# A hybrid decoder trunk on one core: one group of low weight parts on GpSimd, values ahead of the forget gates' transposes, two residual tiles kept, one PSUM buffer and one addition moved

## The chip, the cores and the metric

The kernel runs on one core of a Trainium2 chip. The metric is the device time of one execution in microseconds. Instruction streams of TensorE (PE; PEld is its weight loads), VectorE (DVE), ScalarE (ACT), GpSimd (POOL) and SyncE (SP) run side by side; SyncE and GpSimd issue the DMAs here, each in the order of its queue.

## The reference

Two layers on a sequence of 1024 tokens of width 1024, batch 1, all float32, and a norm at the end. Cut to what matters:

```python
def reference(x, ...):
    for i in range(2):
        h = rms_norm(x, norm_g[i])
        x = x + (lru_mixer(h, ...) if i % 2 == 0 else fox_mixer(h, ...))
    return rms_norm(x, final_g)

def lru_mixer(h, ...):            # width 1536, 12 blocks of 128 channels
    u = h @ w_in                  # branch and gate
    xc = causal_conv(branch)      # 4 taps
    a, b = gates(xc)              # block-diagonal 128x128 products, sigmoids
    y = scan(a, b) * silu(gate)   # h[t] = a[t] h[t-1] + b[t]
    return y @ w_out

def fox_mixer(h, ...):            # 16 heads of 64
    q, k, v, gate, f = split(h @ w_in)
    cum = cumsum(log_sigmoid(f + b_f))
    logits = q k^T / 8 + cum[q] - cum[k], causal
    return (softmax(logits) v * silu(gate)) @ w_out
```

## The kernel before, in words

Products are made of split numbers: a high part and a low part of each operand, and three products (high x high, high x low, low x high) into one PSUM tile. The first layer splits in float32r, the second in float16. The sequence is worked in two halves of 512 tokens (`halves`, `HALF`); a channel block has 128 rows, so a tile of the residual `x` is 128x512.

**First layer**, until about 417 us. Twelve blocks pass through the input products, the convolution, the gates, the scan (`a`), and `outputs`, which makes `yh` and `yl`. Pairs of blocks are projected out by `project_out(g)`. `out_weights` (L396) loads 128x512 weights, has ScalarE make the high part `wh` (`to_hi`) and VectorE the low part `wl` (`to_lo`, L114). Most other low parts of this layer (46 tiles) are made by GpSimd, also in L114.

**The passage** between the layers (about 395 to 500 us, from L670). The last pair's weights are made by four calls of `out_weights`; then for each half the eight residual tiles get their last products (`ops`, L688 adds them to `x`), are stored to `x1d` in DRAM, squared for the norm, and split into the float16 tiles `h` that the second layer's products read. The row of the norm comes by way of small TensorE products (`sscol`, `rsrow`, `xnorm`). Between these, the scheduler places the first products of the second layer: `gps` (queries and keys, gates) and `vps` (values, L798 takes them to `v`). Its order is made by a planner that simulates the program (`schedule_with_timeline_sim`); for a stretch, ScalarE and VectorE keep the order of the code (`manual_schedule`, L1019). The generator `first` gives the values of pair group 0; `take(first, n)` runs n steps of it. The generator `forget` computes the log of the forget gates (`z`, L990), transposes it on TensorE (`fps`, L76), makes the running sum (L998) and stores `decay` rows that the attention loads into `T` and `U`.

**Attention**, about 500 to 976 us. Per head: `S` (scores, TensorE), a masked maximum (L1097, VectorE), exponential (ScalarE), scaling (L1110), a DMA transpose of the probabilities (`pT<-pp`, L1112), `O` (probabilities by values). The order strings at the top say where other work is laid between; from about 887 us this is `partial` (L1256), which multiplies the finished pairs by the output weights, four and two blocks at a time, and adds the residual read back from `x1d` (L1271). `home` (L1241) says where the sum lives: tiles `xh` that stay in SBUF, or, for `db < 3` of the second half (`c == 1`), a pair of buffers `R` (`xp`), from which it goes back to `x1d` (L1273) and is read again at the end (`x1`). Before a load into a buffer that stays, GpSimd copies one column of a tile two steps back (L1266), which makes the load wait for that tile's addition.

**The end** (`turned`, L1302). The residual tiles are transposed into PSUM (`turn`), the last two pairs' output products are added, squares are summed (`ssq`), VectorE multiplies by the gain (L1341), and `root_mean` gives the factor of the norm. For the last rows the gain's product of the last part is issued inside `root_mean` by `between` (L1347). PSUM tiles come from tags with two buffers each: `S`, `g`, `O`; a tile waits until the buffer two allocations back is read.

Of the kernel before, what the change touches and what calls it, by code (L numbers as in the profile page):

```python
# [11 lines left out]
F32 = mybir.dt.float32  # L12
# [5 lines left out]
ALU = mybir.AluOpType  # L18

P = 128  # L20
SEQ = 1024
HALF = 512
KT = 8
NB = 12
# [14 lines left out]
def f32(ap):  # L39
    return ap.bitcast(F32)  # L40
# [3 lines left out]
def trunk(ctx: ExitStack, tc: tile.TileContext, xt, w0, wg, wo0, pc, gn, gf, w1, wv, wf, bf, wo1, out):  # L44
    nc = tc.nc

    def pool(name, bufs, **kw):
        return tc.tile_pool(name=name, bufs=bufs, **kw)
# [5 lines left out]
    ps = ctx.enter_context(pool("ps", 2, space=PSUM))  # L54
# [16 lines left out]
    def matmul(*args, **kw):  # L71
        pe[0] = nc.tensor.matmul(*args, **kw)  # L72
        return pe[0]
# [26 lines left out]
    def to_hi(hi, src, eng, scale=None):  # L100
        if eng is nc.scalar:
            if scale is None:
                cast_last[0] = nc.scalar.copy(hi, src)
            else:
                nc.scalar.activation(hi, src, AF.Copy, scale=scale)
        elif eng is nc.gpsimd:
            nc.gpsimd.tensor_scalar(hi, src, 1.0 if scale is None else scale, 0.0, ALU.mult, ALU.add)
        elif scale is None:
            eng.tensor_copy(hi, src)
        else:  # L110
            eng.tensor_scalar(hi, src, scale, None, ALU.mult)

    def to_lo(lo, src, hi, eng):
        return eng.tensor_tensor(lo, src, f32(hi), ALU.subtract)  # L114
# [3 lines left out]
    def loaded(shape):  # L118

        if spare and next(loads) % 4 == 3:  # L120
            return spare[0].tile([P, *shape], F32, tag="wx", name="wf")
        return wpool.tile([P, *shape], F32, tag="wf", name="wf", bufs=3)
# [30 lines left out]
    def drain(gen):  # L153
        for _ in gen:
            pass

    def take(gen, n):
        for _ in range(n):
            next(gen, None)
# [48 lines left out]
    with nullcontext(ExitStack()) as l0:  # L208
# [43 lines left out]
        first = ([], [])  # L252
# [140 lines left out]
                to_lo(yl, a_, yh, nc.vector)  # L393
            ys.append(y)

        def out_weights(g, d0):  # L396

            wt = loaded([4, P])
            for j in range(2):
                nc.sync.dma_start(wt[:, 2 * j : 2 * j + 2], wo0[d0 + j, :, 2 * g : 2 * g + 2])  # L400
            hi = wpool.tile([P, 4, P], F32R, tag="wh", name="wh")
            lo = wpool.tile([P, 4, P], F32R, tag="wl", name="wl")
            to_hi(hi, wt, nc.scalar)
            to_lo(lo, wt, hi, nc.vector)
            return [[(hi[:, 2 * j + i], lo[:, 2 * j + i]) for i in range(2)] for j in range(2)]

        def project_out(g):
# [76 lines left out]
        for n in range(NB):  # L484
# [3 lines left out]
            else:  # L488
                ups = two_banks("ups")
                both = [ups.rearrange("p a b -> p (a b)")]  # L490
# [61 lines left out]
        rpool = late.enter_context(pool("R", 2, side="right"))  # L552
# [116 lines left out]

        weight_bounds()  # L670
        splitting = iter(())
        wl = [w for d0 in range(0, KT, 2) for w in out_weights(NB // 2 - 1, d0)]
        for h, cs in enumerate(halves):
            y = [tuple(z[:, cs] for z in p) for p in ys[-2:]]
            hT[h] = [hpool.tile([P, 2, HALF], FP16, tag="hh", name="h16") for k in range(KT)]
# [2 lines left out]
            for d0 in range(0, KT, 4):  # L678
# [6 lines left out]
                for db, o in enumerate(pts, d0):  # L685
                    mm3(o, wl[db][1], y[1], False, True)
                    x = xs[h][db]
# [28 lines left out]
    with ExitStack() as l1:  # L716
# [298 lines left out]
        first = values(0)  # L1015
# [26 lines left out]
        one = onesf[:HEADS, :1].to_broadcast([HEADS, HALF])  # L1042
        gates0 = forget(0)
        next(gates0)
        take(first, 3)
        drain(gates0)
        drain(first)
        gw = [None]
# [195 lines left out]
        def home(c, db):  # L1244
            if c == 0:
                x = hpool.tile([P, HALF], F32, tag="hh", name="xh")
            elif db < 3:
                return rpool.tile([P, HALF], F32, tag="R", name="xp")
            elif db < 7:
                x = at.tile([P, HALF], F32, tag="wv", name="xh", bufs=4)  # L1250
            else:
                x = at.tile([P, HALF], F32, tag="wvf", name="xh", bufs=1)
            homes[c, db] = x
            return x
# [24 lines left out]
        def residual(c, q):  # L1279

            cs = slice(q * 256, (q + 1) * 256)
            xs = [homes[c, d][:, cs] if (c, d) in homes else None for d in range(KT)]
            for d in range(0, KT, 2):
                n = xs[d : d + 2].count(None)
                if n:
                    x = wpool.tile([P, 2, 256], F32, tag=("wl", "wh")[q], name="x1")
                    fetch(x[:, :n], x1d[c, :, d : d + n, cs])
                    xs[d : d + n] = [x[:, i] for i in range(n)]
            return xs
# [11 lines left out]
        def turned(c, q):  # L1301


            xs = left.pop((c, q), None) or residual(c, q)

            if c == 0:
                if q:
                    res = [hpool.tile([P, HALF], F32, tag="hl", name="res", bufs=12) for i in range(4)]
                else:
                    res = places_late  # L1310
                res = [res[:2], res[2:]]
            elif q == 0:
                res = [tu.tile([P, SEQ], F32, tag=t, name="res") for t in ("T0", "T1")]
                res = [[z[:, hs] for hs in halves] for z in res]
            else:
                res = at.tile([P, 2, SEQ], F32, tag="pT0", name="res", bufs=1)
                res = [[res[:, b, hs] for hs in halves] for b in range(2)]
            for b in range(2):
                cs = slice(q * 256 + b * P, q * 256 + (b + 1) * P)

                parts = ((0, 4), (4, 2), (6, 2)) if c * q * b else ((0, 4), (4, 4))
                ss = ssq[c][:, 4 * q + 2 * b :][:, : len(parts)]
                for h, (d0, nd) in enumerate(parts):
                    part = res[b][d0 // 4][:, (d0 % 4) * P : (d0 % 4 + nd) * P]
                    pt = ps.tile([P, HALF], F32, tag="gO"[c * b] if h < 2 else "g", name="turn")[:, : nd * P]

                    for i in range(nd):
                        x = xs[d0 + i][:, b * P : (b + 1) * P]
                        matmul(pt[:, i * P : (i + 1) * P], x, ident, start=i == 0, stop=False, is_transpose=True)
                    for k in range(2):  # L1330
                        yh, yl = (z[:, cs] for z in y1[c][6 + k])
                        wh, wl = (z[:, k::2][:, d0 % 4 : d0 % 4 + nd] for z in late_w[d0 // 4])
                        matmul(pt, yh, wh, start=False, stop=False)
                        matmul(pt, yl, wh, start=False, stop=False)
                        matmul(pt, yh, wl, start=False, stop=k == 1)
                        if k == 0:
                            yield
                    sq = at.tile([P, HALF], F32, tag="pp", name="sq1", bufs=4)[:, : nd * P]
                    nc.scalar.activation(sq, pt, AF.Square, accum_out=ss[:, min(h, ss.shape[1] - 1)].unsqueeze(1))
                    if c == 0 or h < len(parts) - 1:  # L1340
                        nc.vector.tensor_tensor(part, pt, grow[d0 // 4][:, (d0 % 4) * P : (d0 % 4 + nd) * P], ALU.mult)  # L1341
                        if h == 1 and c == 1:
                            nc.vector.tensor_tensor(ss[:, 0:1], ss[:, 0:1], ss[:, 1:2], ALU.add)
                            ss = ss[:, 0::2]
                        yield
                if c == 1:
                    r = root_mean(ss, lambda: nc.vector.tensor_tensor(part, pt, grow[d0 // 4][:, (d0 % 4) * P : (d0 % 4 + nd) * P], ALU.mult))  # L1347
                    lo, hi = res[b]
                    nc.scalar.activation(lo, lo, AF.Copy, scale=r)
                    nc.vector.tensor_scalar(hi, hi, r, None, ALU.mult)  # L1350
                    for hs, z in zip(halves, (lo, hi)):
                        nc.sync.dma_start(out[4 + 2 * q + b, :, hs], z)
                    yield
            if c == 0:
                first_half.extend(res)

        def root_mean(ss, between=lambda: None):

            ss = ss.rearrange("p (b h) -> p b h", h=2)
            r = ss[:, :, 0]  # L1360
            nc.vector.tensor_tensor(r, r, ss[:, :, 1], ALU.add)
            between()
            nc.scalar.activation(r, r, AF.Sqrt, bias=eps_o, scale=1.0 / SEQ)
            nc.vector.reciprocal(r, r)
            return r
# [54 lines left out]
        for hd in range(HEADS):  # L1420
# [22 lines left out]
            first, second = LAST if hd > 11 else START if hd == 0 else ORDER  # L1443
            if hd in (4, 8):
                first, second = OPEN
            if hd == HEADS - 1:
                first = "1..1.0.1.0.1..."
# [39 lines left out]
        def finish():  # L1487
# [3 lines left out]
            for i, o in enumerate(first_half):  # L1491
# [4 lines left out]
                yield  # L1496

        run("." * 20, fill=chain(turned(1, 0), turned(1, 1)), side=finish())


# [57 lines left out]
```

## Time and profile before

| | us |
|---|---|
| Median of 3 runs | 1011.85 (1010.98 to 1012.02) |
| The profiled execution | 1012.07 |
| Its span, first to last instruction | 1010.3 |
| TensorE busy in it | 993.2 |
| VectorE | 783.7 |
| ScalarE | 666.3 |
| GpSimd | 163.6 |
| Mean granted TensorE clock | 0.996 |

The profile's page gives busy times, the span in 40 slices, the DMA queues, the chain of work that ended last, and groups of instructions. A bracket behind a row of the timeline is the idle time before the instruction and what ended it. In a row that stands for several instructions (x4), the time is that of all of them together. In rows by stretch, the columns are length, then busy time with count for PE, PEld, DVE, ACT and POOL, the granted clock, the DMA engines' share, and GB/s.

### The profile page before, as it was taken

Reading aid. Unit: us, or ns where it says so; the run is one execution under the profiler, and the core shown is the slowest. Engines: PE = TensorE matmul, PEld = TensorE weight load, DVE = VectorE, ACT = ScalarE, POOL = GpSimd, SP = SyncE. Lnnn points to the kernel's source line nnn. Section 1 sums busy time; section 2 is a strip of 40 time slices with the busy share of each in tenths; the row PEclk is TensorE's granted clock in tenths of the full one; section 3 lists DMA queues with packets and bytes.
Section 4 is the critical chain, followed back from the end, with each engine's and each line's share of the span. In section 5 each row is a group of like instructions: output and inputs, shape, how many; then the busy total and the mean of one; then the engine's idle time right before and its main releaser. Section 6 shows DMA issues by size and latency. Waiting matters only on the chain. (4 is left out here: it accounts for less than half of the span.)

```text
span 1010.3 us, 15178 instructions
## 1 busy us (share of the span) xinstructions
PE 993.2 (98%) x5100; PEld 657.9 (65%) x5100; DVE 783.7 (78%) x1488; ACT 666.3 (66%) x1219; POOL 163.6 (16%) x188
## 2 busy tenths in 40 slices
PE   9999999999999999999999999999999999998997
PEld 6787788888888888776555555555555555443454
DVE  7689685586576567998687988988898879975775
ACT  8469855657657567666775767766676767753555
POOL 1310221221222122000210101101010102422100
PEclk9999999999999999999999999999999999999999
DMA  7111443243333334244277677987777768899944
GB/s 257 62 46 55 126 134 96 93 141 100 119 111 121 104 104 152 64 162 145 49 179 136 142 141 155 176 159 140 130 166 141 163 135 179 180 209 178 185 79 167
DMA packets 214511, 135.89 MB, mean 135 GB/s; under 512 B 162080, under 2 KB 184416, under 8 KB 214432
## 3 DMA queue, kind: packets, MB, share of 16 engines
q1 hardware_dynamic: 206544, 109.48, 46.7%
q0 software_dynamic: 7888, 25.43, 9.4%
q8 instruction: 40, 0.66, 0.3%
q14 instruction: 39, 0.32, 0.1%
HBM read 75.16 MB, written 9.37 MB: 84 GB/s over the span
## 5 line engine op out<-in xcount | busy, mean ns | idle before, releaser
L72 PE MATMUL gps<-h,w 128*128 128x512 f16 x1152 | 267.6, 379 | 0.0
L72 PEld LDWEIGHTS <-w 128*128 128x128 f16 x1440 | 140.3, 98 | 153.9 <-issue 3.5
L60 ACT ACTIVATE p<-p,m 128x128 f32<-128x128 f32 (+7 forms) x128 | 98.7, 771 | 70.9 <-DVE m L1097 67.3
L114 POOL TENSOR_TENSOR wl<-wf,wh 128x512 fp32r<-128x512 f32 x46 | 81.1, 1771 | 317.0 <-ACT wh L60 228.3
L1110 DVE SCALAR_TENSOR_TENSOR pp<-p,sums,pp 128x128 f16<-128x128 f32 (+7 forms) x128 | 104.1, 817 | 19.2 <-ACT pp L60 18.9
L60 ACT ACTIVATE pp<-p,sums 128x128 f16<-128x128 f32 (+7 forms) x128 | 97.0, 769 | 29.8 <-ACT p L60 13.2
L1097 DVE CUSTOM_DVE_ANT_0 p<-S,mask,vsq 128x128 f32<-128x128 f32 (+7 forms) x128 | 103.7, 811 | 15.6 <-PE S L72 15.0
L60 ACT ACTIVATE wsf<-wsf 128x512 f32<-128x512 f32 (+1 forms) x81 | 50.5, 624 | 62.4 <-DMA wsf<-in_w 33.7
L72 PEld LDWEIGHTS <-h 128*128 128x128 f16 x768 | 74.8, 98 | 21.2 <-ACT h L60 1.0
L72 PE MATMUL S<-T,U 128*128 128x512 f16 (+4 forms) x384 | 83.1, 326 | 0.0
L731 POOL DMA_DIRECT2D wf<-in_w x48 | 25.9, 540 | 342.1 <-DVE w L741 159.1
L72 PE MATMUL ops<-yh,wh 128*128 128x512 f32 x192 | 77.1, 402 | 1.7 <-ACT yh L60 1.1
L72 PE MATMUL ups<-hh,wh 128*128 128x512 f32 x192 | 76.5, 399 | 1.2 <-ACT hh L60 1.2
L72 PE MATMUL ups<-hh,wl 128*128 128x512 f32 x192 | 76.2, 397 | 0.8 <-POOL wl L114 0.8
L72 PE MATMUL ops<-yh,wl 128*128 128x512 f32 x192 | 75.7, 394 | 0.8 <-DVE wl L114 0.8
L72 PE MATMUL gps<-hh,wh 128*128 128x512 f32 x192 | 76.0, 396 | 0.0
L72 PE MATMUL gps<-hh,wl 128*128 128x512 f32 x192 | 75.6, 394 | 0.0
L72 PE MATMUL ops<-yl,wh 128*128 128x512 f32 x192 | 74.5, 394 | 0.0
L415 DVE TENSOR_TENSOR x<-x,ops 128x512 f32<-128x512 f32 x80 | 53.7, 679 | 24.3 <-PE ops L72 24.0
L72 PE MATMUL vps<-wv,h 128*128 128x256 f16 x576 | 70.7, 273 | 0.0
L72 PE MATMUL ops<-y,w 128*128 128x512 f16 x288 | 67.8, 384 | 0.0
L60 ACT CAST wh<-wf 128x512 fp32r<-128x512 f32 x72 | 43.6, 610 | 34.5 <-PE ops L72 20.3
(264 smaller groups left out, 1892.2 us busy)
## 6 DMA issues: line engine op xcount, KB each, us to landing
wf<-in_w SPq DMA_DIRECT2D x58, 256.0 KB
wsf<-in_w SPq DMA_DIRECT2D x48, 256.0 KB
wf<-in_w POOLq DMA_DIRECT2D x48, 256.0 KB, 3.5
wf<-in_wo SPq DMA_DIRECT2D x48, 128.0 KB
x<-in_xt SPq DMA_DIRECT2D x16, 256.0 KB
wsf<-in_wv SPq DMA_DIRECT2D x16, 256.0 KB
wsf<-in_wo SPq DMA_DIRECT2D x16, 256.0 KB
x1d<-x SPq DMA_DIRECT2D x16, 256.0 KB
```

What stands on the lines that cost most here:

```text
L60: act[0] = op(*args, **kw)
L72: pe[0] = nc.tensor.matmul(*args, **kw)
L114: return eng.tensor_tensor(lo, src, f32(hi), ALU.subtract)
L415: nc.vector.tensor_tensor(x, x, pt, ALU.add)
L731: by.dma_start(wt[:, :, sl], part)
L1097: nc.vector.tensor_tensor_reduce(p, S[:, :n], mask[:, SEQ - n :], unit_s[:, pair : pair + 1], -NEG, ALU.add, ALU.min, accum_out=m)
L1110: nc.vector.scalar_tensor_tensor(both[:, :, 1], p, r, both[:, :, 0], ALU.mult, ALU.subtract)
```

## The change

1. `out_weights` gets the engine of its low part as an argument, and the four calls at the passage pass GpSimd.
2. `take(first, 3)` ahead of the first half's forget gates becomes `take(first, 8)`: all the values of the second half are issued before the transposes.
3. `home` keeps the tiles of the second half for `db` 1 and 2 in `R`; only `db` 0 goes back to `x1d`. For the two kept tiles the copied column gates the load.
4. One `turn` tile (first half, first quarter, second block, first part) takes a buffer of tag `O` instead of `g`.
5. In `root_mean`, what `between` issues is put behind the addition of `ssq` by a dependency.

```diff
-        def out_weights(g, d0):
+        def out_weights(g, d0, lo_eng=nc.vector):
...
-            to_lo(lo, wt, hi, nc.vector)
+            to_lo(lo, wt, hi, lo_eng)
...
-        wl = [w for d0 in range(0, KT, 2) for w in out_weights(NB // 2 - 1, d0)]
+        wl = [w for d0 in range(0, KT, 2) for w in out_weights(NB // 2 - 1, d0, nc.gpsimd if d0 >= 0 else nc.vector)]
...
-        take(first, 3)
+        take(first, 8)
...
             elif db < 3:
-                return rpool.tile([P, HALF], F32, tag="R", name="xp")
+                x = rpool.tile([P, HALF], F32, tag="R", name="xp")
+                if db == 0:
+                    return x
...
-                    pt = ps.tile([P, HALF], F32, tag="gO"[c * b] if h < 2 else "g", name="turn")[:, : nd * P]
+                    pt = (
+                        ps.tile([P, HALF], F32, tag="O", name="turn")
+                        if c == 0 and q == 0 and b == 1 and h == 0
+                        else ps.tile([P, HALF], F32, tag="gO"[c * b] if h < 2 else "g", name="turn")
+                    )[:, : nd * P]
...
-            nc.vector.tensor_tensor(r, r, ss[:, :, 1], ALU.add)
-            between()
+            both = nc.vector.tensor_tensor(r, r, ss[:, :, 1], ALU.add)
+            with tc.issue_after(both.ins):
+                between()
```

How the order of instructions moves, first on TensorE in the passage, where the last products of the first layer (`ops`, float32r) and the first of the second (`gps`, float16; `gps_3870` keys, `gps_3910` queries) stand together. Before:

```order
1851 L72 LDWEIGHTS w_3875
1852 L72 MATMUL gps_3870<-h_3600,w_3875 128x512
1853 L72 LDWEIGHTS w_3875
1854 L72 MATMUL gps_3870<-h_3600,w_3875 128x512
1855 L72 MATMUL ops<-yh,wh 128x512
1856 L72 MATMUL ops<-yh,wl 128x512
1857 L72 MATMUL ops<-yl,wh 128x512
```

With the change:

```order
1862 L72 MATMUL ops<-yl,wh 128x512
1863 L72 LDWEIGHTS w_3875
1864 L72 MATMUL gps_3870<-h_3600,w_3875 128x512
1865 L72 LDWEIGHTS w_3875
1866 L72 MATMUL gps_3870<-h_3600,w_3875 128x512
1867 L72 LDWEIGHTS w_3915
1868 L72 MATMUL gps_3910<-h_3600,w_3915 128x512
1869 L72 LDWEIGHTS w_3915
1870 L72 MATMUL gps_3910<-h_3600,w_3915 128x512
1871 L72 MATMUL rsrow<-rs_3502,onesf 128x512
1872 L72 MATMUL ops<-yh,wh 128x512
1873 L72 MATMUL ops<-yh,wl 128x512
```

Before, `ops` come back after `gps` at three places, with nine, three and three of them left; with the change at one place, with three left. The two groups of `gps` then alternate. Second, on TensorE at the transposes of the first half's forget gates (`fps`), before:

```order
2310 L72 LDWEIGHTS h_3724
2311 L72 MATMUL vps<-w_3954,h_3724 128x272
2312 L76 MATMUL fps<-ident,z 16x128 x4
2313 L72 LDWEIGHTS h_3724
2314 L72 MATMUL vps<-w_3954,h_3724 128x272
```

With the change:

```order
2347 L72 MATMUL vps<-w_3969,h_3730 128x272
2348 L72 LDWEIGHTS h_3730
2349 L72 MATMUL vps<-w_3969,h_3730 128x272
2350 L76 MATMUL fps<-ident,z 16x128 x4
2351 L72 LDWEIGHTS w_4333
2352 L72 MATMUL gps_4328<-h_3723,w_4333 128x512
```

They stood ahead of the last 19 value products, and stand behind the last. The second half's transposes stand behind 28 products of `gps_4328` instead of 35. Third, on GpSimd, whose queue issues the loads and stores of `partial`, one piece of the difference:

```order
+L1268 COPY xp<-xh 128x1
+L1270 DMA xp<-x1d 128x512
+L731 DMA wf<-in_wo 128x256
+L1275 DMA x1d<-xp 128x512
+L1268 COPY xh<-xp 128x1
+L1270 DMA xh<-x1d 128x512
 L731 DMA wf<-in_wo 128x512
 L731 DMA wf<-in_wo 128x256
-L1273 DMA x1d<-xp 128x512
-L1266 COPY xh<-xp 128x1
-L1268 DMA xh<-x1d 128x512
```

A copy now stands ahead of the load of `xp`; the two later stores `x1d<-xp` are gone from the rest of the queue. Lines from L1246 on are numbered two to seven higher in the changed kernel.

## The prediction

> **What bounds the kernel now.** First the page's engine row and the list of what TensorE waits for:
>
> ```profile
> PE 993.2 (98%) x5100; PEld 657.9 (65%) x5100; DVE 783.7 (78%) x1488; ACT 666.3 (66%) x1219; POOL 163.6 (16%) x188
> ```
> ```profile
> PE O L72 <- DMA pT<-pp: 3.3, 1, 3.3
> ...
> PE turn L72 <- DVE res L1341: 1.2, 1, 1.2
> ...
> PE ops L72 <- DVE wl L114: 0.8, 1, 0.8
> PE vps L72 <- DVE v L798: 0.4, 1, 0.4
> PE ops L72 <- DVE x L688: 0.4, 1, 0.4
> ...
> PE fps L76 <- DVE z L990: 0.3, 1, 0.3
> ```
>
> TensorE is busy 98% of the span. Its matmul count stays as it is, so a gain can only come from its waits, from switches of its operand type, and from what follows the last matmul. The waits shown (columns: total, times, longest) are what this change can touch: 3.3, 1.2, 0.8, 0.4, 0.4 and 0.3 us, one occurrence each. Third, the busy time by stretch around the longest of them, with the chain's longest piece:
>
> ```profile
> 911.77:915.20 3.43, 3.43 (x19) 1.61 (x19) 0.00 (x0) 0.00 (x0) 0.54 (x1) 1.00 1.31 102
> 915.20:918.80 3.60, 0.29 (x4) 0.03 (x1) 0.00 (x0) 0.03 (x1) 0.00 (x0) 1.00 0.95 247
> 918.80:923.00 4.20, 4.20 (x16) 1.61 (x17) 3.40 (x6) 2.39 (x4) 1.64 (x4) 0.59 1.16 221
> ```
> ```profile
> 904.85 13.82 DMA pT<-pp
> ```
>
> The columns after the length are PE, PEld, DVE, ACT and POOL busy, then granted clock, DMA share and GB/s. Two transposes of pT, issued at 904.85, release TensorE only 13.82 us later. VectorE and ScalarE are idle from 911.77, and after the wait the clock is 0.59 for 4.20 us, which costs 4.20 x 0.41 = 1.7 us more. This place costs 3.3 + 1.7 = 5.0 us, more than all the others together.
>
> **Part 1, the low weights on GpSimd.** TensorE's wait of 0.76 us is for the last low part:
>
> ```profile
> 438.72 0.50 PE L72 MATMUL ops<-yh,wl 128*128 128x512 f32 x1 [0.76 <-DVE wl L114]
> ```
> ```profile
> 436.35 0.60 ACT L60 CAST wh<-wf 128x512 fp32r<-128x512 f32 x1
> ```
> ```profile
> 437.98 0.68 DVE L114 TENSOR_TENSOR wl<-wf,wh 128x512 fp32r<-128x512 f32 x1
> ```
> ```profile
> L114 POOL TENSOR_TENSOR wl<-wf,wh x46: 1282/1302/3307, 9.0 to 396.1; 128x512 fp32r<-128x512 f32 x46
> ```
> ```profile
> 394.37 5.07 POOL L114 TENSOR_TENSOR wl<-wf,wh 128x512 fp32r<-128x512 f32 x2 [15.97 <-DMA wsf<-in_wo]
> ```
>
> Its input, the cast, is done at 436.95, and VectorE gets to it a microsecond later, ending at 438.66. GpSimd is free then and starts at about 437.0. At its median of 1.30 us it ends at 438.3, 0.35 us earlier; at 2.53 us (two took 5.07) at 439.5, 0.9 us later; at 3.31 us at 440.3, 1.6 us later. I take no gain and no loss: VectorE is working through two-input instructions at that place, which pulls from the median towards the slow rows. VectorE is rid of 4 x 0.68 = 2.7 us here, which the next wait sees: the 0.4 us for x L688 can shrink by at most itself. I count 0.1, since that add also needs a product that TensorE finishes behind the first wait.
>
> The Trainium skill, "GPSIMD Engine Reference", section "Key points", says that GpSimd shares its SBUF interfaces with VectorE and contends with its instructions of two SBUF inputs. The trace agrees (1.30 us against 2.53 each); by that rule alone the low part would be the slow one, and the sum below would be 0.9 us smaller in gain.
>
> **The new order in the passage, and part 2.** In the order, TensorE goes back from f16 products (gps) to f32 ones (ops) three times before the last ops are done, and once in the changed one. A return costs what these starts show:
>
> ```profile
> 442.27 0.39 PE L72 MATMUL ops<-yh,wl 128*128 128x512 f32 x1
> 442.50 0.40 PE L72 MATMUL ops<-yl,wh 128*128 128x512 f32 x1
> ```
> ```profile
> 451.56 0.60 PE L72 MATMUL gps<-h,w 128*128 128x512 f16 x2
> 451.81 0.58 PE L72 MATMUL ops<-yh,wh 128*128 128x512 f32 x1
> 452.24 0.40 PE L72 MATMUL ops<-yh,wl 128*128 128x512 f32 x1
> ```
>
> After a return the next start is 0.43 us away, without one 0.23; two fewer give 0.4 us. Next the two waits behind it:
>
> ```profile
> 478.96 2.49 PE L72 MATMUL vps<-w,h 128*128 128x272 f16 x17 [0.44 <-DVE v L798]
> ```
> ```profile
> 489.59 0.60 PE L76 MATMUL fps<-ident,z 128*16 128x128 f32 x4 [0.34 <-DVE z L990]
> ```
>
> The first comes while VectorE and ScalarE make values and the second half's h at once. In the changed order the norm's product of the second half (xnorm) stands some ten value products earlier, and VectorE has less to do before it, so I count this wait as gone: 0.44. The transposes fps of the first half go from 19 value products ahead of the end to behind the last. Their z has then had 19 x 0.11 = 2.1 us more (2.49 us hold x17 with the last one's drain, so 0.11 is on the low side of it), and the 0.34 us go. What becomes late is the first half's decay row behind them, by those 2 us, while the second half's transposes come 28 instead of 35 gate products later. Nothing waits for decay in the list above, so its cover is unknown but not nil; if it lacked a microsecond, that microsecond would be lost at the first S. Sum of the passage: 0 + 0.1 + 0.4 + 0.44 + 0.34 = 1.3 us. Bounds: 0.35 + 0.4 + 0.4 + 0.44 + 0.34 = 1.9 above, and 1.3 - 1.6 - 1.0 = -1.3 below.
>
> **Part 3, two residuals kept.** Here the GpSimd queue counts:
>
> ```profile
> 887.89 0.54 POOL L1268 DMA_DIRECT2D xp<-x1d  x1 [2.94 <-DVE gps L786]
> ...
> 905.06 0.54 POOL L731 DMA_DIRECT2D wf<-in_wo  x1
> 906.41 0.54 POOL L1268 DMA_DIRECT2D xp<-x1d  x1 [0.81 <-DMA x1d<-xp]
> 907.47 0.55 POOL L1273 DMA_DIRECT2D x1d<-xp  x1
> ```
> ```profile
> 897.14 0.75 DVE L1271 SCALAR_TENSOR_TENSOR xh<-xh,outs,ops 128x512 f32<-128x512 f32 x1
> ```
> ```profile
> 906.30 0.73 DVE L1271 SCALAR_TENSOR_TENSOR xp<-xp,outs,ops 128x512 f32<-128x512 f32 x1
> ```
> ```profile
> wf<-in_wo POOLq DMA_DIRECT2D x1, 256.0 KB, 12.4
> ```
>
> The write at 907.47 and the one at 921.90 go, and with them half of the later reload. New are two gates: the load of 887.89 must wait for a COPY behind the add that ends at 897.89, so it issues at about 898.5; the load of 906.41 waits for the add of 906.30 to 907.03 and issues at about 907.7, with the weight load behind it. The write of 907.47 stands in the queue while the transposes wait: in the stretch 915.20 to 918.80 the DMA moves 247 GB/s and TensorE stands still. Without its 256 KB that stretch is shorter by 0.262 MB / 247 GB/s = 1.06 us, if the transposes' completion stands behind it; nothing if it does not, since the write is behind most of the loads. The other bound is the whole 5.0 us. I take 0.9, by the row of bytes, which it is nearest to. On the other side the later loads can cost (rival D).
>
> **Part 4, the other PSUM buffer.**
>
> ```profile
> 976.13 0.38 PE L72 MATMUL turn<-wol,y 128*128 128x512 f16 x1
> 977.66 0.66 PE L72 MATMUL turn<-ident,xh 128*128 128x128 f32 x4 [1.16 <-DVE res L1341]
> ```
> ```profile
> 976.93 1.28 DVE L1341 TENSOR_TENSOR res<-turn,grow 128x512 f32<-128x512 f32 x2
> ```
> ```profile
> L1112 SPq DMA_TRANSPOSE pT<-pp x1: 1904/1904/1904, 977.0 to 977.0; - x1
> ```
> ```profile
> 983.70 0.38 PE L72 MATMUL O<-pT,v 128*128 128x256 f16 x2
> ```
>
> The products of 977.66 wait for VectorE to empty a buffer of their tag. With one of tag O, free at that time, they start at about 976.35: 1.2 us. The following tile needs the buffer emptied first at 977.61, just where TensorE now arrives. What could eat the gain is the last transpose: issued over 977.04 to 978.94, it is needed at 983.70 now and at 982.5 then, 3.6 us behind the end of its issue. I count 1.2, and 0 as the lower bound.
>
> **Part 5, the end.**
>
> ```profile
> 1005.13 0.42 DVE L1347 TENSOR_TENSOR res<-turn,grow 128x256 f32<-128x256 f32 x1
> 1005.48 0.15 DVE L1361 TENSOR_TENSOR ssq<-ssq 128x1 f32<-128x1 f32 x1
> 1005.66 0.29 ACT L60 ACTIVATE ssq<-ssq,outs 128x1 f32<-128x1 f32 x1 [0.56 <-DVE ssq L1361]
> 1005.99 0.16 DVE L1364 RECIPROCAL ssq<-ssq 128x1 f32<-128x1 f32 x1 [0.36 <-ACT ssq L60]
> ```
>
> The short add goes ahead of the 0.42 us product, so the root starts 0.3 us earlier; the product ends at about 1005.7 beside it and holds the reciprocal by little. Gain 0.3 us, between 0.2 and 0.35.
>
> **Sum.** 1.3 + 0.9 + 1.2 + 0.3 = 3.7 us, from the profiled execution's 1012.07 to 1008.4; that execution is 0.2 above the median of 1011.85, so 1008.15, rounded to 1008.1.
>
> **Rivals.** A is the forecast, 0.42; its own bounds: passage 0 to 2.0, DMA 0 to 1.1, turn 0.6 to 1.2 make 1007.2 to 1010.9.
>
> B, the slow clock goes, with part of the DMA wait or all of it. The 0.59 stands only behind this longest wait; TensorE's waits of 1.2 us and less show no such stretch. If a wait that is a microsecond shorter leaves the clock whole, the sum grows by 1.7 to 1006.4; if the wait goes altogether, 5.0 stands in place of 0.9: 1008.1 - 4.1 = 1004.0. For it speaks that the load of 887.89 and the writes change the traffic there by half a megabyte and more. Against it: the packets crawl before the write's turn comes, at 102 GB/s from 911.77 with a DMA share of 1.31. 0.22, a third of it for the first form.
>
> The Trainium skill, "TensorE: Matmul & The Clock Gate", section "What's actually happening", halves the clock after an idle window of about 3.4 us. The trace agrees, with 3.3 us of wait ahead of the 0.59; by that rule the first form is what a wait of 2.4 us gives.
>
> C, the gains are hidden: GpSimd's low part at 2.53 us (-0.9), the DMA wait as long as before (-0.9), the turn's 1.2 us given back to the last transpose. What is left is 0.4 + 0.3 = 0.7 us: 1011.2. For it: each of the three has a row that allows it; against it: all must come at once. 0.22.
>
> D, slower: a gated load comes late. The load that moves to 898.5 must be there for the add at 906.30, 7.8 us later; loads of 905.06 took 12.4 us. With that, VectorE would stand from 906.3 to 910.9, and its queue holds the softmax steps (p, sums, pp) that feed the next transposes, so TensorE stands some 4.6 us, with the slow clock's 1.7 behind it: 1008.1 + 0.9 + 6.3 = 1015.3 at worst, 1013.0 with half of the wait. It decides from a landing of about 8 us on. Against it: the same load took 6.9 us when issued at 887.89:
>
> ```profile
> xp<-x1d POOLq DMA_DIRECT2D x1, 256.0 KB, 6.9
> ```
>
> 0.14. That parts 1 or 2 leave the order as it was is excluded by the order itself.
>
> **Numbers.** About 0.2% (2.0 us) is what a measurement of this kernel can tell from no change, so faster begins below 1009.8. A gives 0.39 of its 0.42 to faster, B all of its 0.22, C 0.06: 0.67. Slower is D's 0.14 less 0.03 for landings just too late: 0.11. Same is the rest, 0.22. The range takes in B to its end and the milder half of D: 1003.9 to 1013.0.
>
> **What would show it.** Right: no wait of ops at wl above 0.9 us, none of fps on z, none of vps on v; the turn's wait on res gone from TensorE's list; the chain's piece of pT near 13 us and no write in the queue at 907; the root at the end directly behind the short add. Wrong: a wait of S on T or U (decay late), a wait of xp on its load before L1273, a pT wait moved to another block, a clock below 1.00 in a new place, or O waiting on the last pT near 982.5.

## The result, and the profile after

| six executions each | median us | range |
|---|---|---|
| before | 1010.05 | 1007.26 to 1012.02 |
| with the change | 1005.03 | 1004.56 to 1005.27 |

The ratio is 0.996, with a 95% interval of 0.994 to 0.9979 (here and below such ratios are estimated over the executions and are not the quotients of the two medians). On two other chips, beside the experiments below, the change came to 0.9962 (0.9942 to 0.9982) and 0.9956 (0.9934 to 0.9977). So it is faster by about 0.4%, some 4 to 5 us. The spread matters as much. In this table the kernel before varies by nearly 5 us from one execution to the next, the changed one by 0.7; over 12 executions on each of the other two chips the change spread by 4.4 and 3.9 us, too, and the kernel before by about 12. The profiled execution of before, at 1012.07, lies at the upper end of its spread here.

The list of what TensorE waits for, with the change:

```profile
PE ops L72 <- DVE x L415: 1.1, 1, 1.1
...
PE ops L72 <- DVE x L688: 1.1, 1, 1.1
...
PE ops L72 <- POOL wl L114: 0.4, 1, 0.4
```

The wait of `O` on `pT` (3.3 us), of `turn` on `res` (1.2), of `vps` on `v` and of `fps` on `z` are gone. That on `wl` has halved, to 0.4. Two others have grown: for `x` at L688 from 0.4 to 1.1, and for `x` at L415 from 0.3 to 1.1; in the list of before that one read:

```profile
PE ops L72 <- DVE x L415: 0.3, 1, 0.3
```

The stretch of the partial output products, by ten microseconds:

```profile
910.00:920.00 10.00, 10.00 (x58) 4.87 (x57) 5.29 (x11) 3.82 (x8) 2.58 (x6) 1.00 0.93 232
920.00:930.00 10.00, 10.00 (x50) 4.69 (x49) 9.62 (x20) 6.26 (x11) 2.83 (x5) 1.00 0.61 156
```

TensorE is busy throughout, the clock is 1.00, and the DMA moves 232 GB/s at 910 to 920, where it moved 102 before in the worst part.

To see where the 7.2 us between the two profiled executions come from, the program is cut at instructions that every kernel here has: the first `wnorm` product (start of the passage), the first and the last product of `partial`, the last `turn` product, and the last instruction. Lengths in us, each the difference of two start times in the timeline:

| profiled execution | start to passage | passage and attention | partial products | to the last turn product | end |
|---|---|---|---|---|---|
| before | 416.7 | 471.0 | 84.5 | 32.1 | 5.9 |
| the change | 416.3 | 470.9 | 79.4 | 30.7 | 5.8 |

Of the 7.2 us, 5.1 lie in the stage of `partial`, 1.4 in the turn, and 0.1 in the passage and the attention, where parts 1 and 2 are. The first stage has no edit; over all profiled executions here it lies between 414.9 and 417.8. These are two single executions, and the kernel before has shorter ones: how much of the 5.1 us is the change, and how much the execution that was profiled, the experiments show.

### The profile page after: what moved, and what is told of

It is laid out like the page before. It is cut to its first block, busy times and chain, and to the rows that moved or that the text cites. A ratio compares the mean times of both kernels' runs of the same rounds, so it can differ in the third digit from the quotient of the medians.

```text
span 1003.1 us, 15181 instructions
## 1 busy us (share of the span) xinstructions
PE 990.5 (99%) x5100; PEld 657.3 (66%) x5100; DVE 784.3 (78%) x1484; ACT 665.8 (66%) x1219; POOL 168.4 (17%) x192
## 4 chain that ended last, share of the span: by engine, by line
PE 83%; issue 7%; DMA 3%; DVE 3%; ACT 2%; POOL 1%; SPq 0%; POOLq 0%; ACTq 0%; DVEq 0%
PE gps L72 33%; PE ops L72 17%; PE ups L72 9%; PE vps L72 8%; PE S L72 6%; PE O L72 5%; PE gate L72 2%; DMA wf<-in_w 1%; PE turn L72 1%; POOL wl L114 1%; DMA wsf<-in_wo 1%; DMA x<-in_xt 1%; ACT sq L60 0%; DVE res L1500 0%; DVE x L415 0%
## 5 line engine op out<-in xcount | busy, mean ns | idle before, releaser
L114 POOL TENSOR_TENSOR wl<-wf,wh 128x512 fp32r<-128x512 f32 x50 | 86.7, 1740 | 348.2 <-ACT wh L60 307.4
L415 DVE TENSOR_TENSOR x<-x,ops 128x512 f32<-128x512 f32 x80 | 53.8, 681 | 25.0 <-PE ops L72 24.5
```

Of the source, the lines that this page charges most:

```text
L415: nc.vector.tensor_tensor(x, x, pt, ALU.add)
```

## The experiments

All were timed on one of three chips, each beside many executions of the kernel before: there its median was 1007.53 (first four experiments), 1009.21 (next four) and 1009.58 (last four). The last column of this table counts executions more than 4 us above that kernel's own fastest; three single executions far outside (over 1100 us) are left out of it. The stage lengths are those of the one profiled execution of each kernel. Only that one has a trace, so the last column stands for the long wait by its time alone. The theories A to E of the expectations are not the rivals A to D of the prediction.

| kernel | stores at 903, 907 and 922 us | gates | median us | passage and attention | partial products | over 4 us |
|---|---|---|---|---|---|---|
| before (three chips) | 3 | no | 1007.5, 1009.2, 1009.6 | 471.0 | 84.5 | 44 of 98 |
| part 3 undone | 3 | no | 1005.62 | 470.9 | 84.0 | 3 of 12 |
| part 3 alone | 1 | yes | 1007.24 | 471.2 | 80.2 | 3 of 12 |
| part 1 undone | 1 | yes | 1005.41 | 471.1 | 79.4 | 2 of 12 |
| part 1 by half | 1 | yes | 1004.33 | 470.1 | 79.4 | 1 of 12 |
| the change again | 1 | yes | 1005.47 | 471.0 | 79.4 | 1 of 12 |
| stores doubled | 6 | no | 1015.79 | 470.8 | 87.4 | all 6 over 1013 |
| parts 4 and 5 alone | 3 | no | 1007.80 | 472.6 | 79.5 | 4 of 11 |
| part 1 alone | 3 | no | 1008.98 | 473.2 | 79.4 | 3 of 12 |
| loads added | 3, and 3 loads | no | 1015.02 | 471.2 | 86.6 | 10 of 11 over 1010 |
| gates alone | 3 | yes | 1006.66 | 471.0 | 80.0 | 2 of 12 |
| the change, third time | 1 | yes | 1004.67 | 471.0 | 79.4 | 0 of 12 |
| part 1 by half, again | 1 | yes | 1004.32 | 470.1 | 79.4 | 0 of 12 |

### Part 3 undone

```diff
-                x = rpool.tile([P, HALF], F32, tag="R", name="xp")
-                if db == 0:
-                    return x
+                return rpool.tile([P, HALF], F32, tag="R", name="xp")
```

> The change without part 3: both later stores to x1d back, the two gates gone. Theory A (the stores make the transposes' wait long): the wait of O on pT and the slow clock behind it come back in some executions, as in the kernel before, whose runs lie between 1007.3 and 1012.0; so times spread from 1005 to 1010, with a wait of 2 to 3.5 us in the profile if it falls on such an execution. Theory B (the earlier passage moved the transposes away from the loads, the stores are no cause): times stay at 1005.0 within 0.4 and no wait of O on pT.

Measured: 1003.2 to 1009.69, median 1005.62 (0.997 of before, 0.9953 to 0.9987). The profiled execution is one with the wait. By stretch of 5 us:

```profile
910.00:915.00 5.00, 5.00 (x28) 2.30 (x26) 1.46 (x4) 0.80 (x2) 0.72 (x2) 1.00 1.20 97
915.00:920.00 5.00, 2.23 (x16) 0.90 (x13) 1.25 (x2) 1.97 (x4) 0.00 (x0) 0.91 1.00 251
920.00:925.00 5.00, 5.00 (x22) 2.20 (x21) 3.42 (x6) 1.41 (x3) 2.26 (x5) 0.75 1.22 214
```

It looks as in the kernel before: 97 GB/s at a DMA share of 1.20, then TensorE idle for 2.8 us, then a slow clock. Theory B falls as far as it says that the earlier passage alone is enough. Yet the median is nearly that of the change (1005.47 and 1004.67 on other chips): by their times, most executions get through without the wait.

### Part 3 alone

The same three lines the other way round, in the kernel before.

> The kernel before with part 3 alone. Theory A: all executions lie together, at the fastest of before, 1007.3 within 0.5, with no wait of O on pT. Theory B: the spread of before stays, 1007 to 1012. Theory C (the moved load decides, not the stores): a new wait of VectorE for the load of xp, over 1 us, and no gain.

Measured: 1005.83 to 1014.61, median 1007.24; ratio 0.9997 (0.9976 to 1.0017). Theory A's forecast of no spread falls: 3 of 12 executions lie over the 4 us with part 3, too, and median and spread are those of before, as theory B said. The profiled execution waits 0.7 us for `pT`, and VectorE nowhere waits long for a load of `xp`, so theory C falls as well. Part 3 makes the long wait rarer at most; it doesn't exclude it.

### Stores doubled

```diff
+        x2d = dram.tile([3, P, HALF], F32, name="x2d")
...
                 if (c, db) not in homes:
                     nc.gpsimd.dma_start(x1d[c, :, db], x)
+                    nc.gpsimd.dma_start(x2d[db], x)
```

> The kernel before with each of the three stores to x1d in the last stage issued twice, the second time to another place in DRAM that nothing reads. Theory A: the wait of O on pT comes more often and is longer, median 1009.5 or more, and more than half of the executions 4 us above the fastest. Theory B: the spread and the median of before, 1007.5 within 0.7.

Measured: 1013.68 to 1016.83, median 1015.79, 6.6 us over before on that chip, and none under 1013.

```profile
PE O L72 <- DMA pT<-pp: 5.7, 1, 5.7
```
```profile
910.00:915.00 5.00, 4.85 (x27) 2.10 (x24) 0.06 (x1) 0.38 (x2) 1.36 (x3) 1.00 1.16 82
915.00:920.00 5.00, 0.00 (x0) 0.00 (x0) 0.97 (x3) 0.00 (x0) 0.18 (x1) 0.83 1.07 191
920.00:925.00 5.00, 4.48 (x15) 1.66 (x16) 3.69 (x6) 2.41 (x4) 2.47 (x5) 0.50 1.15 286
```

The wait in the profile is longer, and all six times lie at the long end. This fits theory A, but the edit also adds bytes, and the next one asks whether their direction matters.

### Loads added

```diff
                 if (c, db) not in homes:
                     nc.gpsimd.dma_start(x1d[c, :, db], x)
+                    more = wpool.tile([P, HALF], F32, tag="wl", name="more")
+                    nc.gpsimd.tensor_copy(more[:, :1], x[:, :1])
+                    nc.gpsimd.dma_start(more, x1d[0, :, db])
```

> The kernel before with a load of 256 KB from DRAM into an idle tile behind each of the three stores, where stores_doubled had a second store (a copied column holds it back until the same addition); nothing reads what it loads. Theory A1 (what hurts is stores): near before, median at most 1.5 us above it, and far from the 6.6 us that the doubled stores cost. Theory A2 (any 256 KB more at this place): about 6 us above before, nearly all executions slow, wait of O on pT over 4 us.

Measured: median 1015.02, 5.4 us over before (1.0051, 1.0023 to 1.008), wait 3.8 us:

```profile
910.00:915.00 5.00, 3.85 (x22) 1.66 (x20) 0.00 (x0) 0.00 (x0) 0.00 (x0) 1.00 1.03 104
915.00:920.00 5.00, 2.30 (x10) 0.90 (x11) 3.28 (x7) 3.00 (x5) 1.26 (x3) 0.69 1.14 282
```

Loads hurt nearly as much as stores. Theory A in its narrow form (A1) falls: it is not the direction; 256 KB more in GpSimd's queue while the transposes run does it either way. Both kernels also hold a second wait, which the profile of before doesn't have there: VectorE stands 8.9 us (stores doubled) and 6.3 us (loads added) for its load of `xh`.

```profile
918.96 0.75 DVE L1273 SCALAR_TENSOR_TENSOR xh<-xh,outs,ops 128x512 f32<-128x512 f32 x1 [8.90 <-DMA xh<-x1d]
```
```profile
915.36 0.75 DVE L1271 SCALAR_TENSOR_TENSOR xh<-xh,outs,ops 128x512 f32<-128x512 f32 x1 [6.29 <-DMA xh<-x1d]
```

TensorE's wait ends later in both, with the transposes. Whether the bytes hurt by themselves, or because they put off what stands behind them in the queue, these two runs don't separate.

### Gates alone

```diff
-                if before[-2] is not None and (c, db) in homes:
+                if before[-2] is not None and ((c, db) in homes or (c == 1 and db in (1, 2))):
```

> The kernel before with only the two gates of part 3: the loads of the two xp tiles wait for the copied column, the stores and the reload stay. If the later loads are what helps, few executions are 4 us above the fastest (about 1 in 8, as with part 3); if the stores are what hurts, as many as before (3 or more in 8), median as before within 1.

Measured: median 1006.66 against 1009.58 (0.9975, 0.9953 to 0.9998), 2 of 12 over the 4 us. All stores are there, and only the two loads are issued later: the profiled execution waits 0.4 us for `pT`, and the clock stays whole.

```profile
910.00:915.00 5.00, 4.64 (x26) 2.00 (x23) 0.89 (x3) 0.17 (x2) 0.72 (x2) 1.00 1.07 293
915.00:920.00 5.00, 4.96 (x29) 2.48 (x30) 3.92 (x6) 2.63 (x5) 2.26 (x5) 1.00 1.03 203
```

So the gates, which the prediction had only as a danger, may bring a gain without the saved stores; the interval just leaves out 1, and part 3 alone, which has the same gates and saves the stores besides, showed none. Put together: in kernels without gates 54 of 133 executions lie over the 4 us (the two with added transfers not counted), with gates 9 of 84. The kernel before has more executions, and so a lower fastest one to count from; without it, the count is 10 of 35 against 9 of 84. Five of the seven runs with gates have the other parts, too. All this speaks for a difference in how often the wait comes, not a switch. Which part of it is the gates' is not settled: part 3 alone and part 3 undone have 3 of 12 each on one chip.

### Part 1 undone

```diff
-        wl = [w for d0 in range(0, KT, 2) for w in out_weights(NB // 2 - 1, d0, nc.gpsimd if d0 >= 0 else nc.vector)]
+        wl = [w for d0 in range(0, KT, 2) for w in out_weights(NB // 2 - 1, d0)]
```

> The change with all four low parts back on VectorE. In the profile after, the scan beside GpSimd's low part takes 2.13 us and a squaring sum 1.61. Theory D (GpSimd's instruction stretches VectorE's, and this is what its help costs): the scan is back at 1.28, the wait for x L415 falls from 1.11 to about 0.3 and that for x L688 from 1.1 to 0.4; TensorE's order goes back to three returns (0.4 us) and the wait of vps on v (0.44) comes back, that on wl grows to 0.8. Sum about -1.5 + 1.2: 1004.7, within 0.4 of the change. Rival E (the stretched scan is not on TensorE's path): 1005.5 to 1006.

Measured: median 1005.41, passage and attention 471.1. TensorE's list:

```profile
PE ops L72 <- DVE wl L114: 0.8, 1, 0.8
PE vps L72 <- DVE v L798: 0.7, 1, 0.7
PE gps L72 <- ACT v L60: 0.5, 1, 0.5
PE ops L72 <- DVE x L688: 0.4, 1, 0.4
...
PE ops L72 <- DVE x L415: 0.3, 1, 0.3
```

The two grown waits are back at 0.3 and 0.4, and those on `wl` and `v` are back as well, with one of 0.5 on ScalarE's `v` that the list of before doesn't have. TensorE goes back to `ops` three times again. The stage is as long as in the change (471.0), and the median, 0.7 over theory D's forecast and next to rival E's, lies where the change's does: part 1 as a whole neither gains nor costs. Rival E falls by the waits all the same; theory D has the mechanism right and the balance wrong.

### Part 1 by half

```diff
-        wl = [w for d0 in range(0, KT, 2) for w in out_weights(NB // 2 - 1, d0, nc.gpsimd if d0 >= 0 else nc.vector)]
+        wl = [w for d0 in range(0, KT, 2) for w in out_weights(NB // 2 - 1, d0, nc.gpsimd if d0 >= 4 else nc.vector)]
```

> The change with the first two low parts on VectorE and the last two on GpSimd. The order of TensorE is the one of the change. Theory D: the scan has no GpSimd instruction beside it and takes 1.28, the wait for x L415 falls by 0.8, the rest stays: 1004.2. Rival E: no difference, 1005.0 within 0.2.

Measured: median 1004.33, passage and attention 470.1. The two scans take 2.54 us together, in the change 3.38, and the wait for `x` at L415 is 0.27 instead of 1.11. First the change, then this kernel:

```profile
413.71 3.38 DVE L382 TENSOR_TENSOR_SCAN a<-a,ti 128x512 f32<-128x512 f32 x2
...
417.73 0.50 PE L72 MATMUL ops<-yh,wh 128*128 128x512 f32 x1 [1.11 <-DVE x L415]
```
```profile
412.72 2.54 DVE L382 TENSOR_TENSOR_SCAN a<-a,ti 128x512 f32<-128x512 f32 x2
...
415.89 0.51 PE L72 MATMUL ops<-yh,wh 128*128 128x512 f32 x1 [0.27 <-DVE x L415]
```

Theory D holds in the stage: 0.9 us. For the whole, both kernels once more on one chip:

> The change beside the half form of part 1 on one chip: 1005.2 within 0.4.

> The change with the first two low parts on VectorE: 0.8 under the change on the same chip, as the wait for x L415 (1.1 against 0.3) says; if the scan's stretch were not on the path, no difference.

Measured: 1004.67 (1003.73 to 1007.66) and 1004.32 (1003.46 to 1005.01); ratios to before 0.9956 (0.9934 to 0.9977) and 0.9949 (0.9926 to 0.9971). The change lies 0.5 under its forecast. The stage is again 0.9 us shorter, 470.1 against 471.0; the medians differ by 0.35 instead of 0.8, which the spread of 12 executions doesn't separate from nothing. It is the fastest version here, by the stage rather than by the whole time.

The change itself beside the second four:

> The change itself, on the chip and beside the runs of the other experiments. If the half form of part 1 is the better one, this lies 0.7 above its median of 1004.3, at 1005.0, with the same tail of slower executions. Theory A (stores) expects few executions 4 us above its fastest, as in the other kernels with part 3 (6 in 42); theory B (chance of the transposes' meeting with the loads, no matter which) expects as many as in the kernels without (18 in 53).

Measured: 1005.47, and one execution in 12 over the 4 us, as theory A expected; the change has the gates as well, so this doesn't speak for the stores alone.

### Part 1 alone, parts 4 and 5 alone

Both in the kernel before, with nothing else of the change.

> The kernel before with part 1 alone. Theory D: in the passage the wait for x L415 rises to 1.1 and for x L688 to 1.1, that on wl falls to 0.4 and that of vps on v goes, with one return instead of three; sum -0.3 to +0.3 against before. Rival: the order is worth more than the stretch, 1 us under before.

Measured: 1008.98 against 1009.21 (ratio 1.0016, 0.9998 to 1.0035), passage and attention 473.2, 2.2 us longer than before. Besides the waits for `x` this comes from one that neither theory had, 1.5 us more for `z`:

```profile
PE fps L76 <- DVE z L990: 1.8, 2, 1.5
PE ops L72 <- DVE x L415: 1.5, 3, 1.1
```

With the new order of TensorE the transposes `fps` come too early for their `z`. In the change part 2 puts them behind the last values, and the wait isn't there. Parts 1 and 2 belong together: the second pays what the first breaks.

> The kernel before with parts 4 and 5 alone (the PSUM buffer and the addition). Forecast: the turn's wait of 1.2 us gone, the root 0.3 us earlier: median 1.5 under before, the waits of the passage and the spread unchanged. Rival: the last transpose of pT takes the wait over, median 0.3 under before.

Measured: median 1007.80 (0.9983, 0.9961 to 1.0005), and the stage to the last turn product 30.7 us as in the change, 1.4 below before. The wait of `turn` on `res` is off the list, and no wait on `pT` has come in its place (`O` follows `turn` without a bracket):

```profile
971.68 0.38 PE L72 MATMUL turn<-wol,y 128*128 128x512 f16 x1
971.89 0.38 PE L72 MATMUL O<-pT,v 128*128 128x256 f16 x2
```

That profiled execution has 1.5 us of waits of `S` on its loads, in a stage that the edit doesn't touch, so its passage and attention are longer; of the other profiled executions only loads added has such a wait, of 0.5 us.

Part 1 alone and parts 4 and 5 alone also show what the stage of `partial` takes where part 3 is missing and the long wait doesn't come: 79.4 and 79.5 us, as with the change. At the place where 82 to 104 GB/s flow ahead of the long wait, they and the other profiled executions without it move 234 to 306:

```profile
910.00:915.00 5.00, 5.00 (x25) 2.26 (x24) 3.11 (x10) 2.16 (x6) 1.26 (x3) 1.00 1.16 255
```
```profile
910.00:915.00 5.00, 5.00 (x25) 2.32 (x24) 2.85 (x8) 1.55 (x4) 0.99 (x3) 1.00 1.13 288
```

In part 1 alone GpSimd's queue issues the same load of `xp` and store as before, in the same order; they land after 6.4 and 6.6 us, in the profile of before after 11.8 and 12.1. In these two profiles the stage begins 2.0 and 1.4 us later than in before, as the passage and attention are longer; whether that matters is not shown.

## Why the prediction was right or wrong

The direction and the range held. The time forecast, 1008.1, was 3 us too high. Against the profiled execution from which the sum starts, it lacks 4.2 us in the stage of `partial` and has 1.2 us too much in the passage. That the gain forecast, 3.7 us, lies close to the 3.7 to 5.0 between the medians is in part luck: of the larger terms only the turn's was right as it stood.

**The base.** The sum started from the profiled execution and called it 0.2 us above the median. That execution had the long DMA wait, and by their times the three of the median were of the same sort; of all later executions of the kernel before, about half are 3 us and more below it. A sum made against an execution with that wait forecasts too long a time.

**Part 3, forecast 0.9; 5.1 us less in its stage** between the two profiled executions. Wait and slow clock went together, as in rival B at its far end; the chain's piece of `pT`, which the prediction still expected near 13 us, is not in the chain of the change from 895 to 930 us. But the 5.1 us are what an execution with the long wait loses, not what part 3 saves in each: without part 3 the stage took 79.4 and 79.5 us where the wait didn't come, and 84.0 where it did. What part 3 can give is a rarer wait, and in the median its share was not measured clear of noise: part 3 alone 0.9997 (0.9976 to 1.0017), the rest without it 0.997 (0.9953 to 0.9987). The step that failed is the price of the write by its bytes at 247 GB/s. TensorE stands still in that stretch, but what sets the executions with the long wait apart lies ahead of it, where the transposes and the other queue together get 82 to 104 GB/s; a DMA share above 1 goes with both kinds. What else is in flight bears on it: more loads bring it on as well as more stores, and in the kernels whose loads are issued later it is rarer by the counts. The wait of 2.8 us in part 3 undone already has the slow clock behind it (0.91 and 0.75), the waits of 0.4 and 0.7 have none. So a wait half a microsecond shorter than before's didn't leave the clock whole; whether one of 2.4 us would, as the first form of B has it, no run shows.

**The same gates were rival D's danger.** The two loads that move landed in time: issued at 897.94 and 907.09, they took 3.2 and 5.9 us. D didn't come.

**Part 1's two terms, forecast 0 (with 0.9 and 1.6 as worse cases) and 0.1, measured about -1.2 together.** The forecast asked whether GpSimd's instruction would be slowed by VectorE. It wasn't:

```profile
L114 POOL TENSOR_TENSOR wl<-wf,wh x4: 1275/1286/1302, 414.7 to 437.5; 128x512 fp32r<-128x512 f32 x4
```

All four took 1.28 to 1.30 us, and the wait on `wl` fell by the 0.36 us that the median gave. What was slowed is VectorE. The squaring sum beside the last low part took 1.61 us:

```profile
437.45 1.28 POOL L114 TENSOR_TENSOR wl<-wf,wh 128x512 fp32r<-128x512 f32 x1 [9.13 <-ACT wh L60]
```
```profile
437.67 1.61 DVE L195 TENSOR_TENSOR sq<-sq 128x512 f32<-128x512 f32 x1
...
441.06 0.69 DVE L195 TENSOR_TENSOR sq<-sq 128x512 f32<-128x512 f32 x1
```
```profile
438.78 0.50 PE L72 MATMUL ops<-yh,wl 128*128 128x512 f32 x1 [0.40 <-POOL wl L114]
442.67 0.50 PE L72 MATMUL ops<-yh,wh 128*128 128x512 f32 x1 [1.06 <-DVE x L688]
```

The same sum takes 0.69 us alone. The two waits for `x` grew by 0.84 and 0.67 us, together 1.5, against 0.36 gained: the forecast of 0.1 us for `x` L688 has the wrong sign. The rule that the Trainium skill gives in "GPSIMD Engine Reference", section "Key points" (the two engines contend for SBUF) was weighed on the wrong side: the trace agrees with it, and the engine that pays is the other one.

**The passage, forecast 1.3, measured 0.1.** The parts that were read from the order came as told: one return instead of three (0.4, by the prediction's rows), no wait of `vps` on `v` (0.44), none of `fps` on `z` (0.34). With 0.36 and -1.5 from part 1 the sum is 0.04. Late decay rows cost nothing: no wait of `S` in the change.

**Part 4, forecast 1.2, measured 1.4** as stage, in the change and alone; the last transpose was in time.

**Part 5, forecast 0.3.** From the last product to the start of the root it is 1.34 us before (1004.32 to 1005.66) and 1.13 after (997.24 to 998.37), so 0.2. To the last instruction, kernels with part 5 take 5.7 to 6.1 us and kernels without 5.9 to 6.0: this doesn't show in the whole.

```profile
998.18 0.16 DVE L1367 TENSOR_TENSOR ssq<-ssq 128x1 f32<-128x1 f32 x1
998.25 0.42 DVE L1353 TENSOR_TENSOR res<-turn,grow 128x256 f32<-128x256 f32 x1
998.37 0.29 ACT L60 ACTIVATE ssq<-ssq,outs 128x1 f32<-128x1 f32 x1 [0.35 <-DVE ssq L1367]
```

The sum as measured is 0.1 + 5.1 + 1.4 + 0.1, and 0.4 from the stage without an edit: 7.1 of the 7.2 us between the two profiles. By the stage lengths, between executions that both lack the long wait only the turn's 1.4 us and little else is left; the fastest of 98 executions of before, 1005.06, and of 24 of the change beside them, 1003.73, lie about as far apart. The rest of the 4 to 5 us between the medians would then be the long wait coming less often. What stays open is why a given execution has it, and how the gates, the saved stores and the other parts share in making it rarer. That more traffic beside the transposes brings it on is shown; that later loads make it rarer is likely; what differs between two executions of the same program is not shown.

## What to carry to other kernels

Where executions of one kernel spread by several microseconds, look first whether the profiled one holds a long wait that others don't have, and forecast for the typical one. Work handed to GpSimd isn't free for VectorE: see what VectorE is doing in that microsecond, and move only the pieces that gain more than they slow (here the best form moved the last two of four, though the last one still slowed a squaring sum). When loads are issued may matter as much as how many bytes one saves; here it wasn't settled.

## What the runs showed that was not expected

Between GpSimd and VectorE the instruction that starts second pays, and waits out the first almost fully. In the change a GpSimd low part began at 414.71, ahead of the second of two scans, and the scans took 3.38 instead of 2.54 us; likewise the sum at 437.67 above. Where VectorE was first, GpSimd paid: two low parts begun at 393.80 took 5.40 us instead of 2.6, with VectorE's product of 393.56 and scan of 395.82 at 1.22 and 2.28 us beside them. The same scan of 1024 columns took 3.36 us at 361.01, where a low part had begun at 360.92.

```profile
393.80 5.40 POOL L114 TENSOR_TENSOR wl<-wf,wh 128x512 fp32r<-128x512 f32 x2 [15.70 <-ACT wh L60]
```
```profile
393.56 1.22 DVE L381 TENSOR_TENSOR ti<-ti,m 128x1024 f32<-128x1024 f32 x1
...
395.82 2.28 DVE L382 TENSOR_TENSOR_SCAN a<-a,ti 128x1024 f32<-128x1024 f32 x1
```
```profile
361.01 3.36 DVE L382 TENSOR_TENSOR_SCAN a<-a,ti 128x1024 f32<-128x1024 f32 x1
```

Not every pair does this: the two additions at 417.02, which read a PSUM tile, took their usual 1.25 us with a low part of 1.27 us begun at 417.23 beside them.

```profile
417.02 1.25 DVE L415 TENSOR_TENSOR x<-x,ops 128x512 f32<-128x512 f32 x2
```
```profile
417.23 1.27 POOL L114 TENSOR_TENSOR wl<-wf,wh 128x512 fp32r<-128x512 f32 x1 [1.22 <-ACT wh L60]
```
